# The head of a one-core decoder block: four scale rows made on TensorE, the first weight pairs prepared as they land, and T4's sums placed behind T3

## The chip, the core and the metric

The kernel runs on one core of a Trainium2 chip. A core has five engines with queues of their own that run in parallel and wait for one another by semaphores: TensorE (PE, matrix products, with its weight loads as PEld), VectorE (DVE), ScalarE (ACT), GpSimd (POOL) and SyncE (SP, which here only issues DMA transfers). TensorE accumulates in PSUM, where the kernel uses eight banks of 128 x 512 fp32; everything else lives in SBUF, 128 partitions wide. The metric is device time in microseconds; lower is better.

## The reference, cut to what matters

One layer, 2048 positions, width 1024, all in fp32:

```python
mod = silu(c) @ w_ada + b_ada                  # 3 x 1024
shift, scale, gate = split(mod, 3)
u = x * (1 + scale) + shift                    # 2048 x 1024
h = u @ w_in                                   # q, k, v, attn_gate, pool_in, pool_gate, merge_a, merge_p
a = (sliding_window_attention(q, k, v) * silu(attn_gate)) @ w_attn_proj
p = (group_linear(causal_pool(pool_in)) * pool_scale * silu(pool_gate)) @ w_pool_proj
y = (sigmoid(merge_a) * a + sigmoid(merge_p) * p) @ w_out * (1 + gate)
out = layer_norm(alpha * x + y)
```

The change touches only the first line (shift and scale), the second, and the beginning of the third.

## The kernel before

**Products.** A fp32 operand is held as two parts, `hi` (a rounded copy, made by ScalarE) and `lo` (the rest, made by VectorE). A product of two operands is three matmuls: hi by hi, hi by lo, lo by hi (`mm3`). A product of 256 output rows by 1024 positions is a "quad": Strassen's scheme in Winograd's form, seven half-size products instead of eight. For that, the activations of one half of the sequence (1024 positions) are kept as eight sets, four block quarters (B11, B12, B21, B22) and their sums (T1 to T4), each four tiles of 128 x 512, each with hi and lo. The weights of a quad are a buffer `W` with rooms 0 to 3 and a buffer `A22`; `sum1` and `mid` make W's sums (rooms 1 and 2), `late` changes room 3. `first()` is rooms 0 and 1 (products with B11 and T1), `second()` rooms 1 and 3 (T2 and B21), `third()` rooms 2 and 3 (T3 and B22), and A22 itself goes with T4. `pair_split` makes hi and lo of two rooms on ScalarE and VectorE, in a ring of four buffers.

**Order.** A recording layer keeps each engine's instructions in the order of the source. Quads are worked in groups of two, `front` (B11, T1) and `back` (the rest); `ring` runs the groups and calls a `tick` after each product, at which `hooks` placed by (group, position) put work for other engines. `defer` puts off work by ticks.

**The head** (`head`, from line 1116) is the beginning of the program, before there are any sets. For k from 0 to 7, `load` asks on SP's queue for two rows of the modulation's weights (tile k's shift row and tile k's scale row, 512 KB each) and x's tile k (two halves, the two blocks of 512 positions). For k 0 and 1 the weights of the first and second quad of the first group are asked for behind them. Then, for each k:

- `pe_modulation`: TensorE makes the shift: eight weight loads of 128 x 128, each with a product of one column, from a matrix laid out for it (`wadat`).
- `modulation`: VectorE makes the scale by a multiply-and-reduce over a row of 1024 (`wada`, laid out the other way), and adds TensorE's shift to `mod`.
- `modulate_x`: ScalarE applies both to x's two halves.
- `difference`, `middle`, `closing`: for k 0 to 3, half 1 is B11's tile (`middle`), and the difference of the halves, scaled, T1's tile (`closing`); half 2 goes to DRAM. For k 4 to 7, half 1 is B21's tile, and T2's tile is `ts` minus the scaled part, kept in `ts`. `rest_sums` makes T3's and T4's tile out of `ts` and x.

The products of the first group's first pairs run a tile at a time (`products(i)`: tile i of B11 and T1 for both quads), then those of the second pairs (`more`: T2 and B21). Four banks called mm hold the first pairs' sums, two called lg the second's; pv and pt are two more. `load(k)` is called for all tiles first; the loop `for k in range(2, KT)` then does `opening(k)` (both modulations), `closing(k - 2)`, `middle(k - 1)`, `modulate_x(k)`, and from k 3 to 6 `products(k - 3)`. In k 2 VectorE makes the two quads' `sum1` and `first()` parts, all together. Behind the loop come all sums of T3 and T4 and the parts of T3; the parts of B22 and T4 are left to hooks of the first group (`rest`, positions 4 and 6).

**After the head**, `first_phase` runs the first group's `back` and the other groups of the projections. Its hooks also hold the making of the sets for the other half of the sequence (`sums_to`), from position 4 on.

Of the kernel before, what the change touches and what calls it, by code (L numbers as in the profile page):

```python
# [59 lines left out]
def kernel(  # L60
# [73 lines left out]
    def mm(*args, **kw):  # L134
        pe.matmul(*args, **kw)
# [140 lines left out]
    class Quad:  # L276
# [4 lines left out]
        def __init__(self, srcs, consume):  # L281
            self.srcs, self.consume = srcs, consume

        def load(self, ph, own, q=nc.sync, e=nc.gpsimd):
            self.w, self.a22 = ph.weights(), ph.last(own)
            x = self.w
            q.dma_start(x[:, 2, :], self.srcs[1][:, 0:CH])
            q.dma_start(self.a22, self.srcs[1][:, CH:])
            q.dma_start(x[:, 0::3, :], by_two(self.srcs[0]))
            if e is not None:  # L290
                self.sum1(e)

# [27 lines left out]
    def by_two(t):  # L320
        return t.rearrange("p (a c) -> p a c", a=2)
# [792 lines left out]
    def head(ph):  # L1114

        ct = ph.t.tile([P, KT], F32, tag="ct", bufs=1, name="ct")
        sg = ph.t.tile([P, KT], F32, tag="sg", bufs=1, name="sg")
        cb = ph.t.tile([P, D], F32, tag="cb", bufs=1, name="cb")
        big = kvp.tile([P, 4 * (P + 2 * CH)], F32, tag="kk", name="head_kk")
        small = kvp.tile([P, 2 * (2 * NB + 1) * P], F32, tag="vv", name="head_vv")  # L1120
        early = [pl.tile([P, 4 * D], F32, tag=f"set_{n}", name=f"head_{n}") for n, pl in (("B22", cp), ("T3", ph.t), ("T4", ph.t))]
# [12 lines left out]
        dve.tensor_tensor(ct, ct, sg, ALU.mult)  # L1134
        act.activation(late[0], cb, AF.Sigmoid)
        dve.tensor_tensor(cb, cb, late[0], ALU.mult)
        dve.tensor_scalar(mod[:, KT:], mod[:, KT:], 1.0, None, ALU.add)
        xs, ts, sums, starts = {}, {}, {}, []

        def load(k):  # L1140
            for w, m in zip(ws[k], (k, KT + k)):
                sp.dma_start(w, (wadat if m < KT else wada)[m])
            if k in (0, 1, 6, 7):
                t = ph.spare() if k < 2 else late[k - 6]
                xs[k] = cols(t, 0), cols(t, 1)
# [30 lines left out]
        def opening(k):  # L1176
            pe_modulation(k)
            modulation(k)
# [24 lines left out]

        def rest_sums(i):
            minus(xs[i][0], ts[i], xs[i][0])
            minus(xs[4 + i][0], xs[4 + i][0], ts[i])
# [5 lines left out]
        def products(i):  # L1212
            for w, (a, b, _, _) in zip(starts, opened):
                product(a, w[0], "B11", True, i, i + 1)
                product(b, w[1], "T1", True, i, i + 1)
# [5 lines left out]
        opening(0)  # L1221
        difference(0)
        modulate_x(0)
        opening(1)
        difference(1)
        middle(0)
        modulate_x(1)
# [12 lines left out]

        for k in range(2, KT):
            opening(k)
            if k < 4:
                difference(k)
            if k == 7:
                second_pair(0)
            closing(k - 2)
            middle(k - 1)
            if k == 2:
                for q in grp:  # L1250
                    q.sum1(dve)
                    starts.append(pair_split(ph, q.first(), act, dve))
            modulate_x(k)
            if k in (3, 4):
                grp[k - 3].mid(dve)
            if 3 <= k < 7:
                products(k - 3)
            if k > 5:
                rest_sums(k - 6)
        more(0, "T2", 0, 2)  # L1260
        more(0, "B21", 0, 3)
        closing(6)
        second_pair(1)
        more(1, "T2", 0, 2)
        more(1, "B21", 0, 3)
        middle(7)
# [4 lines left out]
        for i in (2, 3):  # L1271
            rest_sums(i)
        late_sets(cp, "B22")
        late_sets(ph.t, "T3", "T4")
        for i in range(4):
            parts("T3", i, xs[i][0])
        grp[0].late(dve)
        dve.tensor_scalar(nsink, nsink, -1.0, None, ALU.mult)
        rest = [
            lambda name=name, c=c: [parts(name, i, xs[4 + i][c]) for i in range(4)]  # L1280
            for name, c in (("B22", 1), ("T4", 0))
        ]
        return groups, turn, opened, cb, rest

    def first_phase(ph, groups, turn, opened, cb, rest):
# [10 lines left out]
        for i in range(4):  # L1296
# [12 lines left out]
        at(0, 4, lambda: groups[0][1].late(dve))  # L1309
        for n, f in zip((4, 6), rest):  # L1310
# [172 lines left out]
```

## Time and profile before

| | us |
|---|---|
| Three runs, median (lowest, highest) | 1765.89 (1764.87, 1765.94) |
| The profiled execution, time | 1766.12 |
| The profiled execution, span of its instructions | 1764.3 |
| TensorE busy | 1702.9 (97%) |
| VectorE busy | 1206.0 (68%) |
| ScalarE busy | 931.8 (53%) |
| GpSimd busy | 792.7 (45%) |

The profile is of one execution. A row of the timeline has the start, the time from the first to the end of the last of the merged instructions, the engine (with a small q, its queue's DMA issue), the source line, the operation, the output tile and input tiles, shapes, and a count; in brackets, how long the engine had been idle before, and what released it. Names of tiles are shortened: set_B stands for B11, B21 and B22, set_T for T1 to T4, head_B, head_T and head_kk for rooms of the head that hold the modulation's weights. Rows of operations on 1 x 128 columns and the source line L56 are of the recording layer. TensorE's matmuls overlap in the pipeline, so that the distance of starts tells their price, not the time of one.

### The profile page before, as it was taken

The page shows a single profiled execution, that of the slowest core. Times are in us where ns is not written, and L with a number is a line of the kernel's source. Part 1 is how long each engine was busy: PE and PEld are TensorE (multiplying, and loading weights), DVE is VectorE, ACT ScalarE, POOL GpSimd, SP SyncE. Part 2 cuts the span into 40 slices and gives each one's busy share as a digit, 9 for nine tenths or more (in the row PEclk, how much of TensorE's full clock was granted, in tenths as well). Part 3 has the DMA queues.
Part 4 walks back from the last instruction along what each step waited for, and adds up shares of the span by engine and source line. Part 5 has one row for each costly group of instructions (what it writes and reads, how often), then busy time and mean ns, then how long its engine had stood idle before and what let it go on. Part 6 is the DMA issues. An engine that isn't in the chain of part 4 may idle for free. (4 is left out here: it accounts for less than half of the span.)

```text
span 1764.3 us, 24983 instructions
## 1 busy us (share of the span) xinstructions
PE 1702.9 (97%) x8248; PEld 1428.7 (81%) x8248; DVE 1206.0 (68%) x2180; ACT 931.8 (53%) x1969; POOL 792.7 (45%) x618
## 2 busy tenths in 40 slices
PE   6899999999999998999999999999999989999996
PEld 5688888888888887888788888888888768888785
DVE  5967665655777786766655367777867586765777
ACT  4544444545777775454444377777744333423451
POOL 2145454431356567434434125456762562364542
PEclk9999999999999999999999999999999999999998
DMA  9384767743354567687777634544796585689432
GB/s 365 112 279 179 270 210 273 271 148 132 108 173 146 172 219 294 245 281 254 246 274 262 231 98 132 175 155 149 258 356 225 182 257 182 226 314 384 166 143 99
DMA packets 180609, 381.30 MB, mean 216 GB/s; under 512 B 18800, under 2 KB 39296, under 8 KB 180480
## 3 DMA queue, kind: packets, MB, share of 16 engines
q1 hardware_dynamic: 173696, 363.66, 59.2%
q0 software_dynamic: 3552, 11.56, 1.7%
q10 hardware_dynamic: 3232, 4.49, 0.9%
q8 instruction: 65, 1.06, 0.2%
q14 instruction: 64, 0.52, 0.1%
HBM read 244.35 MB, written 138.44 MB: 217 GB/s over the span
## 5 line engine op out<-in xcount | busy, mean ns | idle before, releaser
L56 PE MATMUL mm<-set_B,w_set 128*128 128x512 f32 x3240 | 801.8, 396 | 17.5 <-DVE w_set L132 8.7
L56 PEld LDWEIGHTS mm<-set_B,w_set 128*128 128x128 f32 x3240 | 604.2, 189 | 147.4 <-DVE w_set L132 15.2
L56 PE MATMUL lg<-set_T,w_set 128*128 128x512 f32 x2088 | 505.9, 392 | 14.0 <-DVE w_set L132 8.6
L56 PEld LDWEIGHTS lg<-set_T,w_set 128*128 128x128 f32 x2088 | 390.8, 188 | 103.7 <-DVE w_set L132 14.0
L132 DVE TENSOR_TENSOR w_set<-W,w_set 128x1024 fp32r<-128x1024 f32 x162 | 224.1, 1383 | 175.7 <-ACT w_set L325 171.4
L325 ACT CAST w_set<-W 128x1024 fp32r<-128x1024 f32 x162 | 169.7, 1049 | 242.4 <-PE mm L56 195.6
L56 PE MATMUL mm<-set_T,w_set 128*128 128x512 f32 x1080 | 266.2, 394 | 0.0
L56 PEld LDWEIGHTS mm<-set_T,w_set 128*128 128x128 f32 x1080 | 201.1, 189 | 41.3
L294 POOL TENSOR_TENSOR W<-W,A 128x512 f32<-128x512 f32 x56 | 82.1, 1466 | 221.7 <-DMA W<-in_win_dram 55.9
L303 POOL TENSOR_TENSOR W<-W 128x512 f32<-128x512 f32 x56 | 80.1, 1431 | 155.5 <-DVE w_set L132 143.9
L56 DVE TENSOR_TENSOR o<-pv,o 64x128 f32<-64x128 f32 x256 | 72.4, 283 | 88.3 <-ACT o L56 85.4
L56 ACT ACTIVATE L<-L,nm 128x257 f32<-128x257 f32 (+1 forms) x256 | 127.2, 498 | 9.3 <-DVE nm L56 3.9
L298 POOL TENSOR_TENSOR W<-W 128x512 f32<-128x512 f32 x56 | 88.1, 1574 | 93.8 <-DVE w_set L132 84.7
L56 DVE CUSTOM_DVE_ANT_0 L<-lg,bt,nsink 128x256 f32<-128x256 f32 (+1 forms) x256 | 111.6, 473 | 5.0 <-PE lg L56 0.8
L299 POOL TENSOR_TENSOR W<-W 128x512 f32<-128x512 f32 x56 | 88.1, 1573 | 37.3 <-DMA W<-in_win_dram 28.1
L56 POOL TENSOR_TENSOR w_set<-W,w_set 128x1024 fp32r<-128x1024 f32 x14 | 33.7, 2405 | 139.6 <-ACT w_set L56 97.0
L56 POOL TENSOR_TENSOR p<-nxt,pg 128x512 f32<-128x512 f32 x32 | 42.0, 1311 | 106.4 <-DVE sm L56 102.8
L56 ACT COPY o<-pv 64x256 f32<-64x256 f32 x128 | 47.3, 370 | 78.1 <-PE pv L56 77.3
L56 DVE TENSOR_TENSOR ptl<-pt,pth 128x512 fp32r<-128x512 f32 (+1 forms) x128 | 85.7, 669 | 1.9 <-ACT pth L56 1.7
L56 DVE TENSOR_TENSOR k_lo<-spare,k_hi 128x512 fp32r<-128x512 f32 x61 | 63.2, 1041 | 28.8 <-ACT k_hi L56 15.0
L56 PE MATMUL lg<-kk,qs 128*128 128x256 f32 (+1 forms) x512 | 80.5, 279 | 0.0
L56 ACT ACTIVATE L<-L,sm 128x256 f32<-128x256 f32 (+1 forms) x128 | 64.3, 502 | 29.4 <-DVE sm L56 29.4
(208 smaller groups left out, 2304.9 us busy)
## 6 DMA issues: line engine op xcount, KB each, us to landing
W<-in_win_dram SPq DMA_DIRECT2D x48, 512.0 KB, 5.3
w_set<-wmix_d SPq DMA_DIRECT2D x32, 512.0 KB, 5.2
W<-in_win_dram SPq DMA_DIRECT2D x34, 256.0 KB, 3.4
A<-in_win_dram SPq DMA_DIRECT2D x34, 256.0 KB, 5.0
ag_d<-sig SPq DMA_DIRECT2D x32, 256.0 KB, 3.3
pg_d<-sig SPq DMA_DIRECT2D x32, 256.0 KB, 3.7
ma_d<-sig SPq DMA_DIRECT2D x32, 256.0 KB, 3.9
mp_d<-sig SPq DMA_DIRECT2D x32, 256.0 KB, 3.8
```

The source lines that it names most:

```text
L56: return lambda *args, **kw: self.tc.keep_in_program_order(op(*args, **kw))
L132: engine.tensor_tensor(dst, src, as32(hi), ALU.subtract)
L294: e.tensor_tensor(self.w[:, 1, :], self.w[:, 2, :], self.a22, ALU.add)
L298: e.tensor_tensor(x[:, 1, :], x[:, 1, :], x[:, 0, :], ALU.subtract)
L299: e.tensor_tensor(x[:, 2, :], x[:, 0, :], x[:, 2, :], ALU.subtract)
L303: e.tensor_tensor(x[:, 3, :], x[:, 3, :], x[:, 1, :], ALU.subtract)
L325: a.copy(by_two(hi), raw)
```

## The change

```diff
-        def load(self, ph, own, q=nc.sync, e=nc.gpsimd):
+        def load(self, ph, own, q=nc.sync, e=nc.gpsimd, a12=True):
...
-            q.dma_start(x[:, 0::3, :], by_two(self.srcs[0]))
+            if a12:
+                q.dma_start(x[:, 0::3, :], by_two(self.srcs[0]))
+            else:
+                q.dma_start(x[:, 0, :], self.srcs[0][:, 0:CH])
...
-                sp.dma_start(w, (wadat if m < KT else wada)[m])
+                sp.dma_start(w, (wadat if m < KT or k < 4 else wada)[m])
...
         def pe_modulation(k):
-            sums[k] = bank(("pv", "pt", "lg", "lg")[k % 4])
-            for i in range(KT):
-                mm(sums[k][:, 0:1], ws[k][0][:, i * P : (i + 1) * P], ct[:, i : i + 1], start=i == 0, stop=i == KT - 1)
+            sums[k] = bank(("pv", "pt")[k % 2])
+            for r in range(2 if k < 4 else 1):
+                for i in range(KT):
+                    mm(
+                        sums[k][:, r : r + 1],
+                        ws[k][r][:, i * P : (i + 1) * P],
+                        ct[:, i : i + 1],
...
         def modulation(k):
+            if k < 4:
+                rows = mod[:, 0 : 2 * KT].rearrange("p (r k) -> p k r", r=2)[:, k]
+                dve.tensor_tensor(rows, rows, sums[k][:, 0:2], ALU.add)
+                return
...
             if k < 2:
-                grp[k].load(ph, False, sp, None)
+                grp[k].load(ph, False, sp, None, False)
+            if k in (4, 5):
+                sp.dma_start(grp[k - 4].w[:, 3, :], grp[k - 4].srcs[0][:, CH:])
...
+        def first_pair(x):
+            grp[x].sum1(dve)
+            starts.append(pair_split(ph, grp[x].first(), act, dve))
+
+        def parts_of(k):
+            middle(k)
+            closing(k)
+
+        for k in range(2):
+            pe_modulation(k)
+            difference(k)
+            first_pair(k)
+            modulation(k)
+            modulate_x(k)
+            parts_of(k)
+            grp[k].mid(dve)
...
         for k in range(2, KT):
-            opening(k)
+            if k < 6:
+                products(k - 2, 0)
+            pe_modulation(k)
+            if k < 6:
+                products(k - 2, 1)
             if k < 4:
                 difference(k)
+            modulation(k)
+            modulate_x(k)
+            if k == 6:
+                second_pair(0)
             if k == 7:
-                second_pair(0)
-            closing(k - 2)
-            middle(k - 1)
...
+                more(0, "T2", 0, 1)
+                more(0, "B21", 0, 2)
+                second_pair(1)
+            if k < 4:
+                parts_of(k)
+                continue
+            closing(k - 1) if k > 4 else None
+            middle(k)
...
+        grp[0].late(dve)
+        late_sets(ph.t, "T3")
+        for i in range(4):
+            t3_sum(i)
+            parts("T3", i, xs[i][0])
+        def t4_sums():
+            for i in range(4):
+                minus(xs[4 + i][0], xs[4 + i][0], ts[i])
+            late_sets(ph.t, "T4")
...
+        rest = (0, lambda: grp[1].late(dve)), (4, late_parts("B22", 1)), (5, t4_sums), (6, late_parts("T4", 0))
...
-            steps(hooks, groups, (4, 29, 57, 80)[i], todo)
+            steps(hooks, groups, (7, 30, 57, 80)[i], todo)
```

For tiles 0 to 3, TensorE makes the scale as it makes the shift (the host lays out twelve rows of weights that way instead of eight), and VectorE only adds both columns to `mod`. For tiles 4 to 7 shift and scale are made as before. The first group's weights are asked for without room 3, which comes in a transfer of its own behind x's tile 4 and tile 5. Tiles 0 and 1 are worked right through, each with one quad's `sum1` and first parts, and that quad's `mid` behind. `products(i, x)` does tile i for one quad; quad 0's stands ahead of the modulation of tile i + 2 on TensorE, quad 1's behind it. Tiles 2 and 3 finish their parts in their own round; from tile 4 on `closing` runs one tile behind, where it ran two behind. The second pair of quad 0 is split in round 6 and that of quad 1 in round 7. T3's sums and parts alternate. T4's sums leave the head and stand in the first group's hooks at position 5, B22's parts at 4, T4's parts at 6, and the second quad's `late` at 0 instead of 4. The first two rounds of `sums_to` begin three ticks and one tick later. The rooms that hold the modulation's weights change names (T4, T3, B22 instead of B22, T3, T4).

More of the change, by code (lines that the diff above doesn't have):

```diff
@@ L1120, in head @@
         small = kvp.tile([P, 2 * (2 * NB + 1) * P], F32, tag="vv", name="head_vv")
-        early = [pl.tile([P, 4 * D], F32, tag=f"set_{n}", name=f"head_{n}") for n, pl in (("B22", cp), ("T3", ph.t), ("T4", ph.t))]
+        early = [pl.tile([P, 4 * D], F32, tag=f"set_{n}", name=f"head_{n}") for n, pl in (("T4", ph.t), ("T3", ph.t), ("B22", cp))]
         places = [t[:, i * D : (i + 1) * D] for t in (*early, big) for i in range(4)]
@@ L1155, in pe_modulation @@
         def pe_modulation(k):
-            sums[k] = bank(("pv", "pt", "lg", "lg")[k % 4])
-            for i in range(KT):
-                mm(sums[k][:, 0:1], ws[k][0][:, i * P : (i + 1) * P], ct[:, i : i + 1], start=i == 0, stop=i == KT - 1)
+            sums[k] = bank(("pv", "pt")[k % 2])
[5 more added lines that the diff above has]
+                        ct[:, i : i + 1],
+                        start=i == 0,
+                        stop=i == KT - 1,
+                    )
         def modulation(k):
+            if k < 4:
+                rows = mod[:, 0 : 2 * KT].rearrange("p (r k) -> p k r", r=2)[:, k]
+                dve.tensor_tensor(rows, rows, sums[k][:, 0:2], ALU.add)
+                return
             m = KT + k
@@ L1210, in head, with products @@
         opened = [[bank(), bank(), None, None] for q in grp]
[L1212 to L1215, printed above, removed]
+        def products(i, x):
+            w, (a, b, _, _) = starts[x], opened[x]
+            product(a, w[0], "B11", True, i, i + 1)
+            product(b, w[1], "T1", True, i, i + 1)
         for k in range(KT):
@@ L1241, in head @@
         for k in range(2, KT):
-            opening(k)
+            if k < 6:
[3 more added lines that the diff above has]
+                products(k - 2, 1)
             if k < 4:
                 difference(k)
+            modulation(k)
+            modulate_x(k)
+            if k == 6:
+                second_pair(0)
             if k == 7:
-                second_pair(0)
-            closing(k - 2)
-            middle(k - 1)
[L1249 to L1263, printed above, removed]
+                more(0, "T2", 0, 1)
[6 more added lines that the diff above has]
+            middle(k)
+        more(0, "T2", 1, 2)
         more(1, "T2", 0, 2)
+        more(0, "B21", 2, 3)
         more(1, "B21", 0, 3)
-        middle(7)
         closing(7)
@@ L1270, in head, with late_parts @@
             more(x, "B21", 3, 4)
-        for i in (2, 3):
-            rest_sums(i)
+        grp[0].late(dve)
[7 more added lines that the diff above has]
+            late_sets(ph.t, "T4")
+        def late_parts(name, c):
+            return lambda: [parts(name, i, xs[4 + i][c]) for i in range(4)]
         late_sets(cp, "B22")
[L1274 to L1277, printed above, removed]
         dve.tensor_scalar(nsink, nsink, -1.0, None, ALU.mult)
[L1279 to L1282, printed above, removed]
+        rest = (0, lambda: grp[1].late(dve)), (4, late_parts("B22", 1)), (5, t4_sums), (6, late_parts("T4", 0))
         return groups, turn, opened, cb, rest
@@ L1305, in first_phase @@
             )
-            steps(hooks, groups, (4, 29, 57, 80)[i], todo)
+            steps(hooks, groups, (7, 30, 57, 80)[i], todo)
         for i in range(8):
             steps(hooks, groups, (21, 49, 77, 99)[i // 2] + i % 2, gate_modulation(ph, 2 * KT + i, cb))
-        at(0, 4, lambda: groups[0][1].late(dve))
-        for n, f in zip((4, 6), rest):
+        for n, f in rest:
             at(0, n, f)
```

15 lines of the change are left out of this document (2 added, 13 removed).

## The prediction, made before the changed kernel had run

> **What bounds the kernel now.** I read the page first, then the busy time by stretch, then the timeline of the first 100 us engine by engine, because every line of the change lies before the second group of products.
>
> ```profile
> PE 1702.9 (97%) x8248; PEld 1428.7 (81%) x8248; DVE 1206.0 (68%) x2180; ACT 931.8 (53%) x1969; POOL 792.7 (45%) x618
> ```
> ```profile
> 92.00:1764.00 1672.00, 1635.09 (x7950) 1371.50 (x7948) 1135.73 (x2041) 883.17 (x1890) 772.31 (x569) 0.99 0.62 215
> ```
> After 92 us TensorE is busy 1635.1 of 1672.0 us; 37 us of idle time in 1672 is too little for a delay of the head to be made up, so I let the start of the second group of products (91.70 us, below) stand for the end: what that start gains or loses, the kernel gains or loses. The head is where time can be had. TensorE's timeline there (start, time, operation, tiles, count, idle before and its releaser):
>
> ```profile
> 7.79 3.55 PE L56 MATMUL pv<-ct,head_B 128*128 128x1 f32 x16 [7.79 <-DMA head_B<-in_wadat_dram]
> 14.76 3.57 PE L56 MATMUL pt<-ct,head_B 128*128 128x1 f32 x16 [3.43 <-DMA head_B<-in_wadat_dram]
> 21.32 3.57 PE L56 MATMUL lg<-ct,head_T 128*128 128x1 f32 x16 [2.99 <-DMA head_T<-in_wadat_dram]
> 26.50 3.57 PE L56 MATMUL lg<-ct,head_T 128*128 128x1 f32 x16 [1.61 <-DMA head_T<-in_wadat_dram]
> ```
> ```profile
> 29.93 1.63 PE L56 MATMUL mm<-set_B,w_set 128*128 128x512 f32 x3
> ...
> 35.20 2.14 PE L56 MATMUL pv<-ct,head_T 128*128 128x1 f32 x16
> ...
> 37.98 0.84 PE L56 MATMUL mm<-set_T,w_set 128*128 128x512 f32 x3
> 38.66 0.84 PE L56 MATMUL mm<-set_B,w_set 128*128 128x512 f32 x3
> ...
> 49.11 1.84 PE L56 MATMUL lg<-ct,head_kk 128*128 128x1 f32 x16
> 50.81 0.72 PE L56 MATMUL lg<-set_T,w_set 128*128 128x512 f32 x2
> ...
> 67.63 0.73 PE L56 MATMUL lg<-set_T,w_set 128*128 128x512 f32 x2 [2.84 <-DVE mm L383]
> 69.95 4.13 PE L56 MATMUL lg<-set_T,w_set 128*128 128x512 f32 x10 [1.59 <-DVE w_set L132]
> ...
> 82.19 0.62 PE L56 MATMUL lg<-set_T,w_set 128*128 128x512 f32 x2
> 84.18 5.31 PE L56 MATMUL lg<-set_T,w_set 128*128 128x512 f32 x22 [1.37 <-DVE w_set L132]
> ...
> 91.70 2.60 PE L56 MATMUL mm<-set_B,w_set 128*128 128x512 f32 x10 [1.75 <-DVE w_set L132]
> ```
> The x16 rows are one modulation row of one tile: 16 weight loads, each with a one-column product. To 26.50 TensorE waits for their transfers (the releasers); the first pairs' products begin at 29.93 and end before 49.11; then VectorE's parts release it. The waits that end last are the one before T3 (69.95), 1.37 before T4's second step (84.18), and 1.75 before 91.70.
>
> The same rows give two prices for each TensorE instruction. A modulation row costs 3.43 us early (26.50 to 29.93) and 1.70 later (49.11 to 50.81). Twelve products from 29.93 to 35.20 cost 0.43 each; three from 37.98 to 38.66 cost 0.23 each. The clock's stretches:
>
> ```profile
> 28.99:32.40 3.41, 3.41 (x12) 1.00 1.04 403
> 32.40:35.81 3.41, 3.41 (x12) 1.00 1.03 399
> ...
> 49.47:52.88 3.41, 2.61 (x18) 1.00 0.00 0
> 52.88:56.29 3.41, 3.41 (x9) 0.50 0.00 0
> ...
> 66.53:69.95 3.42, 0.73 (x3) 1.00 0.92 326
> 69.95:73.36 3.41, 3.41 (x8) 0.50 0.74 242
> ```
> (us, TensorE busy, count, granted clock, share and rate of DMA.) The clock column is 0.50 exactly from 52.88 to 56.29 and from 69.95 to 73.36; before the first change, at 35.8, the column says 1.00, but products 0.43 apart are those of 0.50. The changes stand 3.41 us apart or multiples of it. In the stretch before each fall, full-width products filled little: 49.47 to 52.88 has busy 2.61, but of it 1.3 are one-column products (49.11 to 50.81). Stretch 28.99 to 32.40 was busy throughout, over a quarter of it one-column products (to 29.93), and did not open the clock; 32.40 to 35.81, four fifths full products, did. So modulations count as idleness for the clock.
>
> **The change, part by part.**
>
> *Four scale rows on TensorE.* VectorE loses four reductions (1.28 + 0.08 us each, 5.4 in all) and TensorE gains four rows, one each for tiles 0 to 3, queued in order with everything else. VectorE's own rows in the head:
>
> ```profile
> 16.03 1.28 DVE L56 CUSTOM_DVE_ANT_0 head_B<-head_B,cb,mod 128x1024 f32<-128x1024 f32 x1 [3.87 <-DMA head_B<-in_wada_dram]
> ...
> 22.82 1.28 DVE L56 CUSTOM_DVE_ANT_0 head_T<-head_T,cb,mod 128x1024 f32<-128x1024 f32 x1 [3.09 <-DMA head_T<-in_wada_dram]
> ...
> 38.33 0.15 DVE L56 TENSOR_TENSOR mod<-mod,pv 128x1 f32<-128x1 f32 x1
> ...
> 46.42 0.16 DVE L56 TENSOR_TENSOR mod<-mod,lg 128x1 f32<-128x1 f32 x1 [1.06 <-PE lg L56]
> ...
> 47.10 0.75 DVE L56 SCALAR_TENSOR_TENSOR head_B<-head_B,sg,A 128x512 f32<-128x512 f32 x1
> 47.77 0.69 DVE L56 TENSOR_TENSOR set_B<-head_kk,set_B 128x512 fp32r<-128x512 f32 x1
> ...
> 49.57 1.28 DVE L56 CUSTOM_DVE_ANT_0 head_kk<-head_kk,cb,mod 128x1024 f32<-128x1024 f32 x1
> ...
> 51.06 1.22 DVE L56 TENSOR_TENSOR w_set<-W,w_set 128x1024 fp32r<-128x1024 f32 x1
> ...
> 58.43 0.69 DVE L56 TENSOR_TENSOR set_T<-head_B,set_T 128x512 fp32r<-128x512 f32 x1
> 59.04 0.69 DVE L56 TENSOR_TENSOR x<-head_B,x 128x512 f32<-128x512 f32 x1
> 59.64 0.68 DVE L56 TENSOR_TENSOR head_vv<-head_vv,head_B 128x512 f32<-128x512 f32 x1
> ...
> 68.68 1.22 DVE L132 TENSOR_TENSOR w_set<-W,w_set 128x1024 fp32r<-128x1024 f32 x1
> ...
> 77.06 1.79 DVE L56 TENSOR_TENSOR set_T<-head_kk,set_T 128x512 fp32r<-128x512 f32 x1
> ```
> ```profile
> 46.61 1.52 ACT L56 ACTIVATE head_vv<-head_vv,mod 128x512 f32<-128x512 f32 x2 [1.79 <-DVE mod L56]
> 48.03 1.03 ACT L56 CAST w_set<-W 128x1024 fp32r<-128x1024 f32 x1
> ...
> 49.45 0.62 ACT L56 CAST set_T<-head_B 128x512 fp32r<-128x512 f32 x1
> ```
> Two reductions waited for transfers (16.03, 22.82), so their removal buys nothing there. On TensorE both rows of a tile now cost 2 x 3.43 = 6.86 while the clock is closed, which is more than the 5.2 to 6.6 us between the transfers' arrivals (14.76, 21.32, 26.50). So TensorE, which waited for DMA, becomes the bound of this stage. Worked through: tile 0 from 7.79 to 14.6, tile 1 to 21.5 (its rows have landed: 14.76 and 16.03).
>
> *First pairs' sums and parts as they land, products a tile sooner.* ScalarE and VectorE now do tile 0's chain at once: addition, two modulations (1.52), casts, T1's part, ready near 18.5, under TensorE's tile 1. Products of tile 0, pair 0 follow at 21.5 instead of 29.93: six at 0.43, to 24.0. Tile 2's modulation sits behind them, to 30.9; twelve products to 36.0; tile 3's modulation. The half of W that is asked for later (256 KB per pair, two transfers) lets tiles 1 to 3 land 0.7 to 1.3 us sooner, which is worth nothing once TensorE is late; the bytes and the last arrival do not change. Its two new transfers stand in SP's queue before tiles 5 and 6, whose modulations come after 50 us: covered.
>
> From 36.0 on the price hangs on the clock. The twelve products from 30.9 are 5.1 us of full work, enough in most positions of the 3.41 us stretches to open it; tile 3's modulation is then a stretch of idleness, enough to close it again. I take 4.0 for tile 3 (between 3.42 open and 6.86 closed), the next twelve products closed (5.1), and the rest open: to 45.1, tile 4's row to 46.8, twelve products to 49.6, tile 5's row to 51.3, six products to 52.6. Before, that point was 49.11: **3.5 us lost, where products started 8.4 us sooner.** Everything open from 36.0 would have tile 4's row done at 43.8, everything closed at 51.4; both ends are kept.
>
> *Tiles 4 to 7.* Their order on VectorE is changed too: tile k's addition now waits behind the reduction of k, and that behind the last part of tile k-1, and no first-pair work is left to fill those waits. Between additions lie: addition 0.1, two modulations on ScalarE 1.52, ts 0.66 (47.10 to 47.77), B21's part 0.6, reduction 1.28 = 4.2; from tile 5 on T2's cast and part, +1.1 = 5.3; from tile 6 on a pair's cast and low part instead of waiting for T2's cast, 1.0 + 1.13, = 6.9; from tile 7's addition to T2's last part 5.6. Additions: 46.9, 51.3 (TensorE's row), 56.6, 63.5; T2's last part 69.2 against 58.43: 10.8 late.
>
> *T4's sums behind T3.* Before, from 58.43 to T3's start at 69.95 took 11.5 us, in which VectorE made the second half of the eight sums for T3 and T4, and T3's parts. In the changed order eleven VectorE steps lie there: T2's part, W's late difference, sum, a wait of 0.7 for ScalarE's cast, part, sum, addition, second late difference, low part 1.13, part, sum, addition: ten at 0.6 (59.04 to 59.64), 1.13, 0.7 and the handovers, 8.0 in all. T3 starts at 77.2: **7.3 late**, 3.5 regained. Its third and fourth tiles' parts are now made while it runs, so T3's products wait for parts: three waits of up to 0.9, 2.7 us, against the 1.7 that the closed clock cost from 69.95 to 73.36 (half of 3.41): between -1.7 and +1.0, of which I take +1.0, since VectorE has no spare time there.
>
> T4's four sums now lie on VectorE between T3's steps and T4's parts, while GpSimd makes the next group's sums:
>
> ```profile
> 76.47 1.83 POOL L294 TENSOR_TENSOR W<-W,A 128x512 f32<-128x512 f32 x1 [39.34 <-DMA A<-in_win_dram]
> ```
> VectorE's 77.06 row took 1.79 instead of 0.69 and ends 0.55 after this one: two such operations exclude one another. Behind them wait the gates' multiplications and T4's parts, and for those TensorE. Four sums cost 2.4 alone, 7.2 if each meets GpSimd; two and two, 4.8. TensorE's wait at T4 was 1.37; its bounds are 1.4 (all covered) and 8.6, and with T4's parts behind the sums I take 4.2: +2.8. So long a wait can close the clock once (price 1.7), half of it: +0.8. The 1.75 before 91.70 goes, since W's low parts have that time: -1.75.
>
> *The rest* costs nothing: the renamed rooms, the loads of x for the other half behind W's, and hooks three steps later lie beside TensorE's products (97% of the span).
>
> Sum: 7.3 + 1.0 + 2.8 + 0.8 - 1.75 = **+10.15**, on the profiled execution's own 1766.12 (its span of 1764.3 and 1.8 around it; the median shown, 1765.89, is 0.23 lower): **1776.3 us**. Bounds: clock open from 36.0 (-3.0) and T4's sums uncontended (-2.4): +4.8, 1770.9; clock closed to tile 4 (+4.6): +14.8, 1780.9.
>
> **The rivals.**
>
> *The clock opens during the modulations.* The Trainium skill, "TensorE: Matmul & The Clock Gate", Part 1, says that the gate opens after about 3.4 us of sustained busyness and counts no instructions; by an estimate from that page, 14 us of modulations without a gap would open it near 11 to 15 us. The trace speaks against this: 28.99 to 32.40 was busy throughout and stayed closed. Worked from rows: with rows at 1.70 TensorE waits for transfers again, tile 3 is done near 28.5, the first pairs' products end some 4 us sooner than 49.11, but VectorE's chain of tiles 4 to 7 (4.2 + 5.3 + 6.9 + 5.6 = 22.0, where 38.33 to 58.43 was 20.1) and T4's wait (+2.8) give that back: about +3, 1769. Chance 0.08.
>
> *The first products decide (the faster side).* Place: tiles 0 to 3. If a row costs 2.6 us or less, a tile's two rows fit in the 5.2 between arrivals, modulation hides under DMA, and tile 4's addition comes with its transfer. If then T4's sums are covered as well, the 4 us gained at 49.11 reach the end: 1762. For it: VectorE is relieved of 5.4 us in a stretch where it is busy throughout. Against it: the 3.43 of three early rows. Chance 0.06.
>
> *Loss made up at T3.* VectorE is relieved of 5.4 us of reductions and 2.4 of sums ahead of T3; if that, not TensorE's lateness, sets T3's start, 7.8 covers 7.3 and the rest is within noise: 1766. Against it: the reductions of tiles 4 to 7 stay, and each waits for its predecessor. Chance 0.04.
>
> **How the numbers follow.** 0.82 for the forecast (1771 to 1781), 0.08, 0.06 and 0.04 for the rivals. About 0.2%, 3.5 us, is what a measurement of this kernel can tell from no change. Faster 0.06; same 0.08 (the third rival and half of the first); slower 0.86. The range reaches down into the first rival: 1768 to 1781.5.
>
> **What would show it.** Right: TensorE without idle time from 7.8 to near 50, in rows of 32 one-column products of nearly 7 us before 31; first 512-column product near 21.5; T2's last part near 69; T3 near 77; a wait of 3 us or more before T4; second group near 102. Wrong: granted products 0.23 apart before 30 us (first rival), tile 4's row done before 40 (second), T3 at 70 (third). A second group earlier than 95 refutes the whole sum.

## The result, and the profile after

| | us |
|---|---|
| Kernel before, median of 6 runs (lowest, highest) | 1765.85 (1763.29, 1769.07) |
| Changed kernel, median of 6 runs (lowest, highest) | 1776.35 (1770.28, 1777.32) |
| Ratio | 1.0054, 95% interval [1.0042, 1.0067] |
| Profiled execution of the changed kernel, span | 1775.4 (before 1764.3) |

The change made the kernel 10.5 us slower. The predicted time, 1776.3, was met, though, as shown below, two errors cancel in it. The page's line of engines, and all that lies behind the start of the second group (columns as in the prediction's stretches: us, then busy time of PE, PEld, DVE, ACT, POOL, clock, DMA share, GB/s):

```profile
PE 1718.5 (97%) x8312; PEld 1442.2 (81%) x8312; DVE 1193.3 (67%) x2172; ACT 930.1 (52%) x1969; POOL 795.4 (45%) x618
```
```profile
99.00:1775.00 1676.00, 1635.58 (x7950) 1372.33 (x7948) 1133.13 (x2046) 884.57 (x1896) 770.15 (x571) 0.99 0.62 215
```
TensorE's idle time behind the second group is 40.4 us (1676.0 less 1635.58), 3.5 more than before. TensorE's timeline of the head in the changed kernel:

```profile
7.87 6.96 PE L56 MATMUL pv<-ct,head_T 128*128 128x1 f32 x32 [7.87 <-DMA head_T<-in_wadat_dram]
14.68 6.96 PE L56 MATMUL pt<-ct,head_T 128*128 128x1 f32 x32
21.51 1.63 PE L56 MATMUL mm<-set_B,w_set 128*128 128x512 f32 x3
...
24.21 6.82 PE L56 MATMUL pv<-ct,head_T 128*128 128x1 f32 x32
30.90 1.63 PE L56 MATMUL mm<-set_B,w_set 128*128 128x512 f32 x3
...
35.83 4.08 PE L56 MATMUL pt<-ct,head_T 128*128 128x1 f32 x32
39.77 1.63 PE L56 MATMUL mm<-set_B,w_set 128*128 128x512 f32 x3
...
45.03 2.14 PE L56 MATMUL pv<-ct,head_B 128*128 128x1 f32 x16
...
53.09 1.84 PE L56 MATMUL pv<-ct,head_kk 128*128 128x1 f32 x16
54.79 2.55 PE L56 MATMUL pt<-ct,head_kk 128*128 128x1 f32 x16
59.80 2.06 PE L56 MATMUL lg<-set_T,w_set 128*128 128x512 f32 x3 [2.46 <-ACT w_set L56]
...
77.93 2.34 PE L56 MATMUL lg<-set_T,w_set 128*128 128x512 f32 x9 [1.97 <-DVE mm L386]
...
91.58 3.50 PE L56 MATMUL lg<-set_T,w_set 128*128 128x512 f32 x14
95.93 2.57 PE L56 MATMUL lg<-set_T,w_set 128*128 128x512 f32 x10 [0.85 <-DVE w_set L132]
98.33 2.91 PE L56 MATMUL mm<-set_B,w_set 128*128 128x512 f32 x12
```
Behind the first, no row up to 54.79 has idle time in brackets: TensorE is the bound there. Two modulation rows take 6.7 to 6.8 us three times, and 3.94 (35.83 to 39.77) where the clock was open in part. The stretches of the granted clock around it (the column reads 1.00 up to its first recorded change, at 38.82; that the clock was closed before 35.41 is read from the products, 0.44 apart from 30.90 to 34.88):

```profile
35.41:38.82 3.41, 3.41 (x31) 3.32 (x29) 0.00 (x0) 0.00 (x0) 0.00 (x0) 1.00 1.04 411
38.82:45.65 6.83, 6.83 (x22) 5.68 (x21) 2.74 (x5) 2.74 (x5) 0.54 (x1) 0.50 0.88 353
45.65:55.89 10.24, 10.24 (x74) 9.44 (x74) 4.73 (x9) 4.58 (x7) 0.00 (x0) 1.00 0.01 3
55.89:66.13 10.24, 7.31 (x20) 5.02 (x19) 5.74 (x11) 5.92 (x9) 0.00 (x0) 0.50 0.00 1
```
The clock is open after the twelve products from 30.90, closes again at 38.82, within tile 3's rows, and once more at 55.89, behind a stretch that held little but one-column products (from 53.09). VectorE, and GpSimd's first two sums:

```profile
39.95 0.16 DVE L56 TENSOR_TENSOR mod<-mod,pt 128x2 f32<-128x2 f32 x1 [4.64 <-PE pt L56]
...
47.21 0.16 DVE L56 TENSOR_TENSOR mod<-mod,pv 128x1 f32<-128x1 f32 x1 [2.43 <-PE pv L56]
...
54.03 0.69 DVE L56 TENSOR_TENSOR set_T<-head_T,set_T 128x512 fp32r<-128x512 f32 x1 [2.10 <-ACT set_T L56]
...
59.78 1.23 DVE L56 TENSOR_TENSOR w_set<-W,w_set 128x1024 fp32r<-128x1024 f32 x1 [2.52 <-ACT w_set L56]
...
66.67 1.23 DVE L56 TENSOR_TENSOR w_set<-W,w_set 128x1024 fp32r<-128x1024 f32 x1 [2.52 <-ACT w_set L56]
...
69.84 0.69 DVE L56 TENSOR_TENSOR set_T<-head_T,set_T 128x512 fp32r<-128x512 f32 x1
...
87.47 0.69 DVE L56 TENSOR_TENSOR x<-x,head_T 128x512 f32<-128x512 f32 x1
88.07 0.69 DVE L56 TENSOR_TENSOR head_kk<-head_kk,head_T 128x512 f32<-128x512 f32 x1
88.67 1.29 DVE L56 TENSOR_TENSOR head_vv<-head_vv,head_T 128x512 f32<-128x512 f32 x2
89.88 0.68 DVE L547 TENSOR_TENSOR sig<-sig,mm 128x512 f32<-128x512 f32 x1
...
94.08 0.69 DVE L547 TENSOR_TENSOR sig<-sig,mm 128x512 f32<-128x512 f32 x1
```
```profile
85.61 5.53 POOL L297 TENSOR_TENSOR W<-W,A 128x512 f32<-128x512 f32 x1 [43.12 <-DMA A<-in_win_dram]
91.22 4.10 POOL L302 TENSOR_TENSOR W<-W 128x512 f32<-128x512 f32 x1
```
Two kinds of waits: for TensorE's modulation (4.64, 2.43), and for ScalarE's cast of what VectorE is to finish next (2.10, 2.52, 2.52). The second kind is the lost look-ahead: nothing of another tile stands between a cast and the part behind it.

### The profile page after: what moved, and what is told of

Read it like the earlier page. It is cut to its first block, busy times and chain, and to the rows that moved or that the text cites. A ratio compares the mean times of both kernels' runs of the same rounds, so it can differ in the third digit from the quotient of the medians.

```text
span 1775.4 us, 25127 instructions
## 1 busy us (share of the span) xinstructions
PE 1718.5 (97%) x8312; PEld 1442.2 (81%) x8312; DVE 1193.3 (67%) x2172; ACT 930.1 (52%) x1969; POOL 795.4 (45%) x618
## 5 line engine op out<-in xcount | busy, mean ns | idle before, releaser
L297 POOL TENSOR_TENSOR W<-W,A 128x512 f32<-128x512 f32 x56 | 86.7, 1549 | 216.8 <-DMA A<-in_win_dram 60.6
```

The source lines that it names most:

```text
L297: e.tensor_tensor(self.w[:, 1, :], self.w[:, 2, :], self.a22, ALU.add)
```

## The experiments

All runs compare one mark: the third product of the second group on TensorE (91.70 before; in a merged row of twelve it lies two spacings of 0.23 behind the start, so 98.80 in the changed kernel).

| run | mark, us | against 91.70 | median (runs) | kernel before beside it | ratio, interval |
|---|---|---|---|---|---|
| changed kernel | 98.80 | +7.1 | 1776.35 (6) | 1765.85 | 1.0054 [1.0042, 1.0067] |
| c_before | 91.95 | +0.25 | 1767.31 (10) | 1765.21 | 1.0009 [1.0000, 1.0018] |
| u_scale | 95.34 | +3.6 | 1772.97 (5) | 1765.21 | 1.0044 [1.0031, 1.0056] |
| a_scale | 95.88 | +4.2 | 1771.84 (5) | 1765.21 | 1.0038 [1.0025, 1.0051] |
| u_skew | 94.04 | +2.3 | 1770.62 (7) | 1765.21 | 1.0030 [1.0019, 1.0041] |
| u_skew_scale | 88.88 | -2.8 | 1765.53 (12) | 1764.82 | 1.0000 [0.9990, 1.0010] |
| u_t4 | 99.95 | +8.2 | 1777.78 (6) | 1764.82 | 1.0072 [1.0055, 1.0088] |
| u_skew_scale_t4 | 92.10 | +0.4 | 1768.58 (12) | 1764.82 | 1.0016 [1.0002, 1.0029] |
| a_tail | 92.60 | +0.9 | 1768.48 (12) | 1764.44 | 1.0021 [1.0011, 1.0031] |
| u_open | 107.17 | +15.5 | 1782.84 (6) | 1764.82 | 1.0096 [1.0078, 1.0113] |
| u_keep | 108.22 | +16.5 | 1783.58 (6) | 1764.44 | 1.0123 [1.0099, 1.0147] |
| u_keep2 | 90.40 | -1.3 | 1777.29 (11) | 1769.89 | 1.0039 [1.0025, 1.0054] |
| u_skew_keep2 | 85.14 | -6.6 | 1770.14 (12) | 1769.89 | 1.0005 [0.9985, 1.0025] |

**c_before: the same kernel again.**

> The kernel before once more, as the yardstick for two traces of one kernel. If the start of the second group stands for the end, as the prediction had it, this trace has its second group within 0.3 us of 91.70 and its later products keep whatever shift they have there, within 1 us, up to the end. If executions of one kernel drift apart by themselves behind the second group (the changed kernel is 7 us late there and 11 at its end), the later products of this trace wander by some 2 to 4 us against the first one.

Its mark is 0.25 late, its span 1.0 longer, its median 2.1 over the runs beside it. So a median here is good to some 2 us, whatever its interval says, and the mark is the sharper measure of what an edit does to the head. Behind the mark the two traces of this one kernel drift apart by up to 2.6 us (at 680 us) and come back to 0.9. The mark says nothing, though, of what comes behind it, and the drift there is as large as several of the differences below.

**u_scale: the four scale rows back on VectorE.**

```diff
-                sp.dma_start(w, (wadat if m < KT or k < 4 else wada)[m])
+                sp.dma_start(w, (wadat if m < KT else wada)[m])
...
-            for r in range(2 if k < 4 else 1):
+            for r in range(1):
...
-            if k < 4:
-                rows = mod[:, 0 : 2 * KT].rearrange("p (r k) -> p k r", r=2)[:, k]
-                dve.tensor_tensor(rows, rows, sums[k][:, 0:2], ALU.add)
-                return
```


> The changed kernel with the four scale rows back on VectorE and all else left as it is. Theory A (TensorE late: a second modulation row of 3.4 us for each of four tiles under a closed clock delays the first pairs' products, 3.5 us of the sum): the last of those products moves from 52.4 to about 49, T2's last part from 69.8 to about 66.5, the second group from 98.3 to about 95, the time from 1776.3 to about 1773. Theory B (the order on VectorE and ScalarE behind the products sets the loss, TensorE's lateness is swallowed by it): the last product moves by the same 3 us, T2's last part by less than 1, the time stays at 1775.5 to 1776.5.

The mark came back by 3.5, T2's last part by 5.0 (69.84 to 64.85):

```profile
64.85 0.69 DVE L56 TENSOR_TENSOR set_T<-head_T,set_T 128x512 fp32r<-128x512 f32 x1
```
Theory A's size, and not theory B's nothing. But 3.6 of the 7.1 remain at the mark.

**a_scale: the same rows alone, on the kernel before.**

```diff
-                sp.dma_start(w, (wadat if m < KT else wada)[m])
+                sp.dma_start(w, (wadat if m < KT or k < 4 else wada)[m])
```
(and the two-row `pe_modulation` and addition of the change)

> The kernel before with the four scale rows on TensorE alone: no other edit of the change. Theory A: four more rows of 3.4 us put 13.7 us on a TensorE that had 5.2 to 6.6 us between arrivals and one row of 3.4 in them; the last first-pair product ends some 3.5 us behind its 49.1, the second group starts at about 95.2, the time is 1769.4 (3.5 over before). Theory B: the rows are hidden (the products' end moves, but VectorE, freed of some 2 us for each tile, makes it up), the second group stays within 1 us of 91.7 and the time within 1 us of before.

```profile
21.60 13.79 PE L56 MATMUL lg<-ct,head_T 128*128 128x1 f32 x64
35.25 1.63 PE L56 MATMUL mm<-set_B,w_set 128*128 128x512 f32 x3
```
Eight rows without a gap, 27.4 us from 7.85 to 35.25, all closed; the first product is 5.3 us later than the 29.93 of before, the mark 4.2 (3.9 over c_before). Theory A again: of 5.3, the 5.4 us of reductions taken from VectorE gave back 1.1 at most.

**u_skew: the order of before for tiles 4 to 7.**

```diff
-            modulate_x(k)
-            if k == 6:
-                second_pair(0)
-            if k == 7:
-                more(0, "T2", 0, 1)
-                more(0, "B21", 0, 2)
-                second_pair(1)
...
-            closing(k - 1) if k > 4 else None
-            middle(k)
-        more(0, "T2", 1, 2)
+            if k == 7:
+                second_pair(0)
+            if k > 5:
+                closing(k - 2)
+            if k > 4:
+                middle(k - 1)
+            modulate_x(k)
+        more(0, "T2", 0, 2)
+        more(0, "B21", 0, 3)
+        closing(6)
+        second_pair(1)
...
-        more(0, "B21", 2, 3)
...
+        middle(7)
```


> The changed kernel (scale rows on TensorE, T4's sums behind T3's) with the first pairs' work of tiles 4 to 7 in the order of before: closing two tiles behind, the middle one behind, the later products of T2 and B21 behind the loop. Theory A: T2's last part comes at about 69 as in the changed kernel, since the products are as late as there; the second group at 97.5 to 98.5; the time 1775.5 to 1776.5. Theory B: the chain between additions (4.2, 5.3, 6.9, 5.6 us in the prediction) goes, 4 to 7 us of it come back: T2's last part at 63 to 66, the second group at 92 to 94.5, the time 1769.5 to 1772.5.

```profile
57.61 0.15 DVE L56 TENSOR_TENSOR mod<-mod,pt 128x1 f32<-128x1 f32 x1
57.68 1.22 DVE L56 TENSOR_TENSOR w_set<-W,w_set 128x1024 fp32r<-128x1024 f32 x1
...
64.37 0.69 DVE L56 TENSOR_TENSOR set_T<-head_T,set_T 128x512 fp32r<-128x512 f32 x1
```
The pair's part at 57.68 follows the addition with no wait, where the changed kernel has 2.52; T2's last part is 5.5 earlier, the mark 4.8. So theory B is right as well, and A was not the whole. The edit moves three things at once (the parts of tiles 4 to 7, the second pairs' splits and their first products); which of them is worth what was not tested.

**u_skew_scale: both undone.** (The two edits above together.)

> The changed kernel with both undone that gave time back one at a time: the four scale rows on VectorE (third product of the second group 95.34 instead of 98.80, 3.5 us) and the order of before for tiles 4 to 7 (94.04, 4.8 us). Theory A+B (TensorE's lateness and the lost look-ahead are two causes that add up): third product of the second group at 98.8 - 3.5 - 4.8 = 90.5, within 1 us, the time 1764 to 1767, as before. Rival (they are one cause, each edit removes the same wait): no better than the better of them, 93 to 95, the time 1769 to 1771.

9.9 earlier at the mark, 1.6 more than 3.5 + 4.8 and outside the 1 us that was allowed: two causes and not one, and more than their sum, for which no trace gives the reason. What is left of the change then puts the mark 2.8 us *ahead* of before's, in a time that is the same as before's: of the 2.8, 1.7 are gone by 145 us.

**u_t4 and u_skew_scale_t4: T4's sums ahead of T3's again**, in the changed kernel and in the last one.

```diff
+        for i in range(4):
+            minus(xs[4 + i][0], xs[4 + i][0], ts[i])
...
         def t4_sums():
-            for i in range(4):
-                minus(xs[4 + i][0], xs[4 + i][0], ts[i])
```


> The changed kernel with T4's four sums ahead of T3's again, all else left. The prediction had its place as a cost (T4's wait 4.2 us instead of 1.37, and 0.8 of a closed clock): if so, T4's products come without a wait, the second group 2 us or more earlier than in the changed kernel (third product at 96.8 or below), the time 1773 to 1774.5. Rival (the move paid: it takes 4 sums of 0.69 us, 2.7 us, from in front of T3, and the 0.85 us wait at T4 is less than before's 1.37): T3 starts 2 to 2.7 us later than 77.93, the third product is at 98.5 to 101, the time 1776 to 1779.

> The changed kernel with the scale rows on VectorE, the order of before for tiles 4 to 7, and T4's sums ahead of T3's: what is left of the change is the first pairs' sums and parts as they land, and their products a tile sooner. If that remainder is free (or pays), the third product of the second group is at 88.5 to 91.7 and the time 1763 to 1766. If the remainder costs by itself (first pairs' parts in front of the modulation on VectorE and ScalarE), it is at 92.5 or later and the time 1767 or more.

```profile
75.17 0.74 PE L56 MATMUL lg<-set_T,w_set 128*128 128x512 f32 x2 [1.33 <-DVE mm L386]
81.19 4.63 PE L56 MATMUL lg<-set_T,w_set 128*128 128x512 f32 x10 [5.28 <-DVE w_set L132]
...
93.97 5.67 PE L56 MATMUL lg<-set_T,w_set 128*128 128x512 f32 x24
```
T4's 24 products now run without a wait, as the prediction's term would have it, but T3 stands 5.28 us behind the weights' low part, and the mark is 1.1 later (3.2 in the other pair). At the mark the move paid; the prediction had booked a loss. (In time only the second pair tells the two kernels apart, 1765.53 and 1768.58.) And what is left when all three are undone, the early first pairs with T3's alternating sums and the later hooks, brought nothing: 92.10, with c_before at 91.95.

**a_tail: the tail of the change alone, on the kernel before**: T4's sums behind T3's, T3's sums alternating with its parts, `late` and the hooks as in the change.

```diff
-            if k > 5:
-                rest_sums(k - 6)
...
-        for i in (2, 3):
-            rest_sums(i)
+        grp[0].late(dve)
+        late_sets(ph.t, "T3")
+        for i in range(4):
+            t3_sum(i)
+            parts("T3", i, xs[i][0])
...
-        late_sets(ph.t, "T3", "T4")
-        for i in range(4):
-            parts("T3", i, xs[i][0])
-        grp[0].late(dve)
```
(and `t4_sums` with the hooks of the change)

> The kernel before with the tail of the change alone: T4's sums behind T3's, each T3 sum ahead of its part, the first late gate sum ahead of them. Theory D (this edit pays by itself, against the prediction's +2.8 for it: 3.2 us in the pair of the changed kernel with and without it where scale rows and order were as before, 88.9 against 92.1): third product of the second group at 88 to 89.5, the time 1762 to 1764. Rival (it pays only where the first pairs are early, as in that pair): third product at 91 to 93, the time 1765 to 1767.

```profile
68.51 0.74 PE L56 MATMUL lg<-set_T,w_set 128*128 128x512 f32 x2 [0.64 <-DVE set_T L56]
74.82 0.79 PE L56 MATMUL mm<-set_B,w_set 128*128 128x512 f32 x1 [5.57 <-ACT set_B L56]
```
The rival's mark: no gain, and a time (1768.48) above the rival's 1765 to 1767. T3 begins at 64.92, but T4's sums and casts now stand ahead of B22's on ScalarE and VectorE, and TensorE waits 5.57 for the first part of B22. Neither this edit (92.60) nor the early first pairs without the move of T4's sums (92.10) gain on c_before's 91.95; together they gain 3.1 (88.88).

**u_open, u_keep, u_keep2: is it the clock?** Products that nobody reads, to open it and keep it open.

> The changed kernel with products that nobody reads (the identity by itself, 128x128, into a bank that is free then): 10 of them ahead of tile 0's modulation, 8 inside each of the modulations of tiles 0 and 1, 4 inside those of tiles 2 and 3. Theory (the rows take 3.43 us because the clock is closed, and full-width work opens it): clock open before 8 us, a row at 1.75 us plus its idle products, first pairs' first product at 17 to 18 instead of 21.5, last one at about 49 instead of 52.4, second group 3 us earlier (third product at about 95.5), time about 1773. Rival (such products don't open the clock, or the clock is not why a row takes 3.43): rows as slow as before, 24 idle products of 0.6 us in their way, 14 us of which some 8 lie in front of the first pairs' products: third product beyond 102, time above 1780.

```profile
0.26:3.68 3.42, 2.33 (x11) 2.33 (x12) 1.02 (x33) 1.70 (x3) 1.03 (x7) 1.00 0.48 97
3.68:7.09 3.41, 2.31 (x11) 2.01 (x10) 0.00 (x0) 0.23 (x1) 0.00 (x0) 1.00 0.80 217
```
The ten idle products filled 2.33 and 2.31 us of the two stretches of 3.41 that they fell in, 68% at most, and the clock stayed closed. The rival's number, but the theory was not put to the test. So wider ones, for u_keep:

```diff
+        warmth, wide = bank("lg"), sets["T2"][:, 3, 0, :]
...
+        def idle_product():
+            mm(warmth, wide[:, 0:P], wide, start=True, stop=True)
+        for i in range(14):
+            idle_product()
...
+                    if k < 2 and i not in (2, 6):
+                        idle_product()
+                if 2 <= k < 4:
+                    products(k - 2, r)
...
-            if k < 6:
+            if 4 <= k < 6:
                 products(k - 2, 0)
```
(`wide` is 128x512 in the rounded form, four copies of the identity. The edit also moves products of the first pairs in between the two rows of tiles 2 and 3, so it changes more than the clock.)

> The changed kernel with full-width products that nobody reads, 128x512 in the fast form this time (0.43 us under a closed clock, so that whole 3.4 us stretches are full): 14 ahead of tile 0's modulation, 6 in each modulation row of tiles 0 and 1, and for tiles 2 and 3 the first pairs' products put between the two rows. The run with small idle products left the clock closed and tested nothing. Theory (closed clock makes the rows 3.4 us, full-width work opens it): the clock is open before 10 us, a row takes 1.7 us beside its products, the last first-pair product comes at 46 to 49 instead of 52.4, the third product of the second group at 94.5 to 96.5 as with the scale rows on VectorE, the time at 1771 to 1774. Rival 1 (clock opens, but the order on VectorE behind the products takes up the gain): last product early, third product still at 98 or later, the time 1776 or more. Rival 2 (the rows do not follow the clock): rows at 3.4 us, third product beyond 101.

The operand's place (T2's last tile) was not free before 20 us, so the whole head began 18.4 us later (first modulation at 26.29). In itself it showed the clock open for 41 us without a break (products 0.23 apart from 25.1, the first closed stretch at 66.06). With the operand in B11's last tile, written first:

> The run with wide idle products again, their operand now written into a place that is free from the start (in the last run it came free at 20 us, so that all began 19 us late; from its first modulation at 26.3 to the end of its last at 64.5 it took 38.2 us under an open clock, against 49.1 in the changed kernel, 7.9 to 57.0). Theory (the closed clock holds the rows at 3.4 us): clock open before 10 us, the last modulation done at 45 to 49 instead of 57.0, the third product of the second group 5 to 10 us before the changed kernel's 98.8, at 89 to 94, the time 1766 to 1771. Rival (TensorE's time is worth no more than the 3.5 us that came back with the scale rows on VectorE, the rest is the order on VectorE): third product at 95 to 97, the time 1772 to 1774.

```profile
2.36 5.52 PE L56 MATMUL lg<-set_B 128*128 128x512 f32 x14 [2.36 <-DVE set_B L56]
7.71 0.28 PE L56 MATMUL pv<-ct,head_T 128*128 128x1 f32 x2
...
20.56 1.84 PE L56 MATMUL pv<-ct,head_T 128*128 128x1 f32 x16
22.26 0.94 PE L56 MATMUL mm<-set_B,w_set 128*128 128x512 f32 x3
...
44.59 1.92 PE L56 MATMUL pt<-ct,head_kk 128*128 128x1 f32 x16 [0.33 <-DMA head_kk<-in_wadat_dram]
49.88 2.06 PE L56 MATMUL lg<-set_T,w_set 128*128 128x512 f32 x3 [3.37 <-ACT w_set L56]
```
```profile
47.74:54.56 6.82, 4.65 (x10) 3.25 (x11) 4.36 (x7) 3.91 (x7) 0.00 (x0) 0.50 0.00 0
```
A modulation row by itself takes 1.70 (20.56 to 22.26). In tiles 0 and 1 the six idle products in each row take most of that back: four rows from 7.71 to 20.56 are 3.2 each, against 3.4 in the changed kernel, so the gain lies in the tiles behind. The last row is done 10.8 us sooner (46.5 against 57.3), the mark 8.4. The clock closes first at 47.74, behind the last modulations, when no full product had run since 42.4. The theory holds at the mark; its rival, 95 to 97, does not. The time is another matter: 1777.29 in the median, though the traced execution took 1766.87; the eleven runs went from there to 1780.96. The time goes with the mean granted clock: 0.989 or 0.990 in the four runs up to 1772.44, 0.980 to 0.987 in the seven from 1776.85 on. By an estimate from these figures, 0.005 less in the mean over 1770 us is 18 us more at half clock, which costs up to 9 us of products. Why the clock was lower in these executions no trace shows, since only the one of 1766.87 was traced. The kernel before beside them stood at 1769.89 (1764.4 to 1765.9 in the other sets), at a clock of 0.988 to 0.993.

**u_skew_keep2: with the order of before as well.**

> The same idle products, and the order of before for tiles 4 to 7; scale rows on TensorE, T4's sums behind T3's. If the three costs (closed clock 5 to 10, order 4.8) add: third product of the second group at 84 to 89, the time 1760 to 1765, below the kernel before for the first time. Rival (what binds is the arrival of the tiles and VectorE, as with the scale rows on VectorE, 88.9 and 1765.5): 88 to 90 and 1764 to 1767.

```profile
85.30:1762.20 1676.90, 1635.74 (x7951) 1371.76 (x7949) 1133.90 (x2046) 885.36 (x1896) 769.92 (x571) 0.99 0.63 215
```
The mark adds up, 85.14, 6.6 us ahead of the kernel before; the traced execution took 1764.23, and TensorE idled 41.2 us behind the mark, 4.3 more than in the kernel before. So most of the 6.6 was lost behind the mark. Twelve runs spread from 1761.15 to 1779.65, and again by the granted clock: the five at 0.989 or 0.990 took 1761.15 to 1765.13, the seven at 0.983 to 0.986 took 1769.67 to 1779.65. The kernel before beside them took 1765.15 to 1772.92. It beats the changed kernel's median; that it beats the kernel before is not shown, since nothing here says what decides the clock of a run.

## Why the prediction was right, and where it was not

- *TensorE late.* Right in its steps: first product 21.51 (21.5), tile 3's rows 3.94 (4.0), first pairs' products done 53.09 (52.6). Undone, it returned 3.5 at the mark (term 3.5). The reason given, one-column products that leave the clock closed, holds: u_keep2 has the same rows at half their price under an open clock.
- *Tiles 4 to 7.* Additions at 47.21, 51.78, 57.11, 63.99 (46.9, 51.3, 56.6, 63.5), T2's last part at 69.84 (69.2). The lost look-ahead is half of what the two edits undone together return: 4.8 of 9.9 by itself.
- *T3.* Start 77.93 (77.2): 8.0 late for 7.3. From there to T4's first product 13.65 (77.93 to 91.58), 12.24 before: +1.4 for +1.0. (Of the 1.4, 0.45 is counting: before, two of T3's products had run at 67.63, so 48 products lie in the 13.65 and 46 in the 12.24.)
- *T4: the step that failed.* "with T4's parts behind the sums I take 4.2: +2.8", and +0.8 for the clock. T4's wait was 0.85, less than the 1.37 of before, and the clock stayed open. The four sums took 0.69 each; it was GpSimd that was held, 5.53 us for its first sum (5.61 to the start of its second). So it was in the seven other runs that have the sums there behind early first pairs: 3.37 to 5.56 us, with a wait of 0.83 to 0.85 at T4 in all eight traces. The bound of 1.4 was the true end, and the mechanism the wrong way round: -0.5 for +3.6. The 1.75 behind it went as forecast.
- *"The start of the second group stands for the end."* 8.0 + 1.4 - 0.5 - 1.75 = 7.1 at the mark, where 10.15 was forecast; the span grew by 11.1. So 4 us came behind the mark, 3.5 of it as idle time of TensorE. The prediction had argued that a delay could not be made up there, and did not ask whether it could grow. c_before's trace has 1.4 more idle time there too (0.75 of growth in its span) with no change at all, so the part that belongs to the change is some 2 to 3 and is not traced to a cause. Product by product the changed kernel is 7.1 late at the mark, 8.2 at 145 us, 9.3 from 360 to 636, 7.1 again from 975 to 1290, and 10.2 at 1750: what was added by the end arose behind 1290, where TensorE's waits of over 0.15 us come to 13.5, against 11.4 and 11.7 in the two traces of the kernel before. The right total is luck: 3.6 + 0.5 too much in the T4 term, 4 unforeseen behind, and 1.1 of small misses ahead.
- *"The rest costs nothing."* Not so at one place. The eleven traces with the tail and hooks of the change lose 0.4 to 2.8 us between the mark and 145 us, the two without them (c_before, a_scale) less than 0.1. In the changed kernel it is 1.1, with a wait of 0.18 for VectorE's multiplication in the gates; since the kernel is back at 7.1 later, what this costs at the end is not shown, and no run has the hooks alone. In u_scale, where it is 2.8, the same wait is 2.00:

```profile
138.78 2.99 PE L56 MATMUL lg<-set_T,w_set 128*128 128x512 f32 x12 [2.00 <-DVE p L408]
```
- *Rivals.* The clock did not open during 14 us of back-to-back modulations (6.96 and 6.96 for two rows each), against the rule that the first rival took from the Trainium skill, "TensorE: Matmul & The Clock Gate", Part 1. The second rival's mechanism, rows of 2.6 or less, was real but had to be made, and brought the mark to 90.4 (u_keep2), not the time to 1762. The third had no part.

## What to carry to other kernels

Before moving small work onto an engine that idles, see at what clock it will run: here one-column products with little else among them ran at half the clock. Under an open clock a row cost half, 1.70 for 3.43, and full-width products among the rows kept it open. Useless ones opened it but cost nearly what they saved in their own rows (3.2 against 3.4 with them in); the gain came in the rows behind, among products that were needed anyway. Where a chain goes through two engines for each tile, the tiles in flight are the buffer: working each tile right through to start earlier cost 4.8 us at the mark here, and the earlier start by itself returned nothing. Measure the head by a mark in the trace, and run the old kernel once more, before trusting an interval of 0.1%. But do not take the mark for the time: marks 2.8 and 6.6 us ahead came out at the old kernel's median.

## What the hardware showed that was not expected

- The clock changed only at the ends of stretches of 3.41 us, and what filled a stretch went with the change. In u_open a stretch filled to 68% left the clock closed; in u_keep2 one filled throughout (3.36 to 6.78) opened it, and the twelve stretches behind it, with six or more full products of 0.23 to each row up to 42.4, were open. The Trainium skill, "TensorE: Matmul & The Clock Gate", Part 1, speaks of sustained busyness; here TensorE was busy without a gap from 7.87 to 35.41 and closed.
- Which engine is held was not to be foreseen. GpSimd's first sum took 5.53 us beside VectorE's row of 0.69 us steps, and VectorE's steps kept their 0.69; in the kernel before, VectorE's 77.06 row was the one that waited (1.79), though VectorE ran back to back there too (rows at 75.86, 76.46 and 77.06), so no rule of who wins comes out of these traces. Both of GpSimd's long rows end 1.25 us behind the start of VectorE's next instruction with an operand in PSUM (89.88 and 94.08, which read a bank mm). The Trainium skill, "SBUF — State Buffer", Who interferes with whom, has the second to issue blocked until the first finishes; here GpSimd's row spans eight whole instructions of the other engine, not one.
